# Loading part of one tile in transfers of 12, 8, 8, 4 and 96 partitions in a DMA-bound gradient kernel

## The chip, the core and the metric

The kernel runs on one core of a Trainium2 chip. The metric is the device time of one execution in microseconds; the lower, the better. A core has compute engines (here VectorE, called DVE, and GpSimd, called POOL, do the arithmetic), a sync engine SP that issues the transfers, and 16 DMA engines that move data between the device memory (HBM) and the on-chip memory (SBUF, 128 partitions).

## What is computed

```python
x = randn(8192, 8192).astype(float32)
return np.gradient(x, axis=1)
```

Along each row of 8192 numbers, an inner element of the result is half the difference of its right and left neighbours. The first and the last element of a row are plain differences: second minus first, and last minus last but one. Input and output have 268.4 MB each.

## The kernel before

The 8192 rows are cut into `nsets` = 32 tiles (sets) of 256 rows. A partition holds `R` = 2 neighbouring rows of one tile, one after the other: `W` = 16384 numbers, 64 KB. So a tile is 128 partitions of 64 KB, 8.39 MB, and is contiguous in HBM (L36 and L37). There are `NB` = 3 buffers in SBUF, `slot0` to `slot2` (L40); tile i uses slot i % 3. The input is put `SH` = 64 numbers from the start of the buffer and the result is written from its start, so that the result of a tile takes the place of its input.

For each tile the steps are these.

- **Load**, `load(i)` (L58 to L61): one DMA of the whole tile, issued by SP (L60). From tile 3 on it waits for the store of the tile that had the same slot, `stores[i - NB]`.
- **Row ends** (L70): POOL takes the one-sided differences at the two ends of each row, 128 x 4 numbers, into the small tile `ends`. It waits for the load.
- **Inner elements** (L76): one DVE instruction over the whole tile, 128 x 16382, halves the differences of neighbours. It waits for the row ends, because it overwrites the input.
- **Placing the ends** (L87): DVE or, in 12 of the 32 tiles, POOL copies the row ends into the result.
- **Store** (L89): one DMA of the whole tile, issued by SP. It waits for the placing.

All loads and stores are issued by SP, in the order in which the program has them: loads 0, 1, 2, then stores 0, 1, 2, loads 3, 4, 5, stores 3, 4, 5 and so on, up to loads 30 and 31 and stores 30 and 31 (L91 to L93 issue the next three loads after each third store). An instruction that waits at SP holds those behind it. The order is written out by hand (`tc.manual_schedule()`), and `chain` (L45) tells the framework which waits each step needs: the named steps, and the instruction before it on its engine where both belong to the same slot. Each transfer reports its completion on one of eight semaphores, which are taken in turn; a transfer that takes a semaphore again also waits for the transfer that had it eight issues earlier.

Of the kernel before, what the change touches and what calls it, by code (L numbers as in the profile page):

```python
# [1 line left out]

# [4 lines left out]


@with_exitstack
def kernel(  # L10
    ctx: ExitStack,
    tc: tile.TileContext,
    x: bass.AP,
    out: bass.AP,
):

    nc = tc.nc
    P = nc.NUM_PARTITIONS
    n, m = x.shape
    R = 2
    NB = 3  # L30
    SH = 64
    W = R * m
    nsets = n // (P * R)
    f32 = x.dtype

    x_sets = x.rearrange("(s p t) m -> s p (t m)", p=P, t=R)  # L36
    out_sets = out.rearrange("(s p t) m -> s p (t m)", p=P, t=R)  # L37

    pool = ctx.enter_context(tc.tile_pool(name="pool", bufs=1))
    slots = [pool.tile([P, SH + W], f32, name=f"slot{k}", tag=f"slot{k}") for k in range(NB)]  # L40
    ends = pool.tile([P, nsets, R, 2], f32, name="ends", tag="ends")
    loads, stores = [], [None] * nsets
    in_front = {}

    def chain(i, ins, *needed):  # L45

        group, engine = f"slot{i % NB}", ins.ins.engine
        keep = [o.ins for o in needed]  # L50
        if in_front.get(engine, (None,))[0] == group:
            keep.append(in_front[engine][1])
        tc.declare_no_dep(ins.ins, group=group, keep=keep, reason="implied by the needed step")
        tc.add_to_no_dep_group(group, ins.ins)
        in_front[engine] = group, ins.ins
        return ins

    def load(i):  # L58
        b = slots[i % NB]
        ins = nc.sync.dma_start(out=b[:, SH : SH + W], in_=x_sets[i])  # L60
        loads.append(chain(i, ins, *([stores[i - NB]] if i >= NB else [])))  # L61

    with tc.manual_schedule():
        for i in range(NB):
            load(i)
        for i in range(nsets):
            b = slots[i % NB]
            xin = b[:, SH : SH + W].rearrange("p (t m) -> p t m", m=m)

            ins = nc.gpsimd.tensor_sub(  # L70
                out=ends[:, i, :, :],
                in0=xin[:, :, 1 : m : m - 2],
                in1=xin[:, :, 0 : m - 1 : m - 2],
            )
            at = [chain(i, ins, loads[i])]
            ins = nc.vector._custom_dve(  # L76
                dve_ops.TENSOR_TENSOR_REDUCE_SUB_MAX,
                out=b[:, 1 : W - 1],
                in0=b[:, SH + 2 : SH + W],
                in1=b[:, SH : SH + W - 2],  # L80
                s0=0.0,
                s1=0.5,
            )
            halved = chain(i, ins, *at)
            res = b[:, 0:W].rearrange("p (t m) -> p t m", m=m)
            placer = nc.gpsimd if i % 5 in (1, 3) and i < nsets - 2 else nc.vector
            ins = placer.tensor_copy(out=res[:, :, 0 : m : m - 1], in_=ends[:, i, :, :])  # L87
            placed = chain(i, ins, halved)
            ins = nc.sync.dma_start(out=out_sets[i], in_=b[:, 0:W])  # L89
            stores[i] = chain(i, ins, placed)  # L90
            if i % NB == NB - 1:  # L91
                for k in range(i + 1, min(i + 1 + NB, nsets)):
                    load(k)  # L93


# [1 line left out]
_INS = ['x']  # L97
_OUTS = [((8192, 8192), 'float32')]


# [23 lines left out]
```

## Time and profile before

| | |
|---|---|
| median of 3 runs | 1247.86 us (1247.71 to 1247.9) |
| span of the profiled execution | 1245.7 us |
| HBM read and written | 268.44 MB each |
| L76, DVE, 32 times | 551.2 us, 17.224 us each |
| L70, POOL, 32 times | 6.3 us, 0.198 us each |
| L87, DVE 20 times, POOL 12 times | 3.4 us and 2.3 us |
| loads, L60, 32 times | 0.339 us to issue; 58.0 us from issue to landing (median) |
| stores, L89, 32 times | 0.343 us to issue; 40.4 us from issue to landing (median) |
| loads 0, 1 and 2 have landed at | 22.7, 42.0 and 62.4 us |

The span goes from the first to the last instruction in the profile; the times of the runs are measured from outside and are some 2 us longer. A transfer's time to landing includes its time in the queue behind earlier transfers. The trace also holds a record for each DMA packet: its start, its duration and its size, but not the DMA engine that it ran on. A load or a store of a whole tile leaves 128 packets of 65,536 bytes (one for each partition) and 16 of 4 bytes, which report the completion of each of the 16 engines.

### The profile page before, as it was taken

To read this page: it belongs to the slowest core of one execution; us is meant where nothing else is said; L and a number is where in the kernel's file an instruction comes from. 1 tells how busy PE (TensorE), PEld (TensorE's weight loads), DVE (VectorE), ACT (ScalarE), POOL (GpSimd) and SP (SyncE) were. 2 spreads that over 40 slices of the span, in tenths; PEclk is the share of its full clock that TensorE was granted. 3 is DMA by queue.
4 is the path that set the end of the run, shared out by engine and by line. 5 is a ranking of instruction groups with operands and counts; after the bars stand their busy time and mean duration, and the time that the engine had idled before them with its cause. 6 is when DMAs were issued, how large, how long until landed. Compare 5 with 4: busy or idle time off the path is not lost.

```text
span 1245.7 us, 237 instructions
## 1 busy us (share of the span) xinstructions
DVE 554.6 (45%) x52; POOL 8.8 (1%) x48
## 2 busy tenths in 40 slices
DVE  2850583069009702850582079009603840591083
POOL 0000000000000000000000000000000000000000
DMA  9999999999999999999999999999999999999999
GB/s 404 438 436 423 427 431 438 438 438 436 436 427 431 425 438 436 425 434 436 429 434 436 434 436 434 436 434 438 419 436 436 434 438 438 431 434 429 429 410 404
DMA packets 9217, 536.88 MB, mean 431 GB/s; under 512 B 1024, under 2 KB 1024, under 8 KB 1024
## 3 DMA queue, kind: packets, MB, share of 16 engines
q1 hardware_dynamic: 9216, 536.88, 99.8%
q14 instruction: 1, 0.01, 0.0%
HBM read 268.44 MB, written 268.44 MB: 431 GB/s over the span
## 4 chain that ended last, share of the span: by engine, by line
another core or an unknown queue 74%; DVE 18%; DMA 3%; issue 2%; POOL 1%; SPq 0%; POOLq 0%
DVE slot L76 18%; DMA slot<-in_x_dram 3%; POOL ends L70 0%; POOL slot L87 0%; SPq L60 0%; POOLq L119 0%; DVE slot L87 0%
## 5 line engine op out<-in xcount | busy, mean ns | idle before, releaser
L76 DVE CUSTOM_DVE_ANT_0 slot<-slot 128x16382 f32<-128x16382 f32 x32 | 551.2, 17224 | 668.7 <-POOL ends L70 668.7
L70 POOL TENSOR_TENSOR ends<-slot 128x4 f32<-128x4 f32 x32 | 6.3, 198 | 989.6 <-DMA slot<-in_x_dram 989.6
L87 POOL COPY slot<-ends 128x4 f32<-128x4 f32 x12 | 2.3, 190 | 207.9 <-DVE slot L76 207.9
L87 DVE COPY slot<-ends 128x4 f32<-128x4 f32 x20 | 3.4, 172 | 0.7
L108 POOL MEMSET const-bfloat16-1.0<- 128x1 bf16 x1 | 0.1, 101 | 0.0
L108 POOL MEMSET const-uint8-127<- 128x1 uint8 x1 | 0.1, 101 | 0.0
L108 POOL MEMSET const-float32-0.0<- 128x1 f32 x1 | 0.1, 98 | 0.2 <-issue 0.2
L108 POOL MEMSET const-float32-1.0<- 128x1 f32 x1 | 0.1, 98 | 0.0
## 6 DMA issues: line engine op xcount, KB each, us to landing
slot<-in_x_dram SPq DMA_DIRECT2D x32, 58.0
out_dram<-slot SPq DMA_DIRECT2D x32, 40.4
```

Of the source, the lines that this page charges most:

```text
L70: ins = nc.gpsimd.tensor_sub(out=ends[:, i, :, :], in0=xin[:, :, 1 : m : m - 2], in1=xin[:, :, 0 : m - 1 : m - 2],)
L76: ins = nc.vector._custom_dve(dve_ops.TENSOR_TENSOR_REDUCE_SUB_MAX, out=b[:, 1 : W - 1], in0=b[:, SH + 2 : SH + W], in1=b[:, SH : SH + W - 2],
L87: ins = placer.tensor_copy(out=res[:, :, 0 : m : m - 1], in_=ends[:, i, :, :])
L108: nc = _bacc.Bacc("TRN2", target_bir_lowering=False, num_devices=1)
```

## The change

Tile 2, the third, is loaded in six transfers instead of one. The last `STEP` = 4096 columns of its 16384 (16 KB of the 64 KB in each partition) are cut off and loaded by five transfers, of partitions 0 to 11, 12 to 19, 20 to 27, 28 to 31 and 32 to 127. A sixth transfer loads the first 12288 columns (48 KB) of all 128 partitions. They are issued by SP in this order, in the place where the one load of tile 2 was. POOL's first step on tile 2 waits for all six. All other tiles are loaded as before, in one transfer, and the stores and the arithmetic are the same.

```diff
+    STEP = 4096
...
     def load(i):
         b = slots[i % NB]
-        ins = nc.sync.dma_start(out=b[:, SH : SH + W], in_=x_sets[i])
-        loads.append(chain(i, ins, *([stores[i - NB]] if i >= NB else [])))
+        after = [stores[i - NB]] if i >= NB else []
+        parts = []
+        whole = W
+        if i == NB - 1:
+            whole = W - STEP
+            first = 0
+            for k in (12, 8, 8, 4, 96):
+                parts.append((slice(first, first + k), slice(whole, W)))
+                first += k
+        parts.append((slice(0, P), slice(0, whole)))
+        loads.append([])
+        for rows, cols in parts:
+            ins = nc.sync.dma_start(
+                out=b[rows, SH + cols.start : SH + cols.stop], in_=x_sets[i][rows, cols]
+            )
+            loads[i].append(chain(i, ins, *after))
...
-            at = [chain(i, ins, loads[i])]
+            at = [chain(i, ins, *loads[i])]
```

The instructions of DVE and POOL and their order are the same in both programs. SP has 69 transfers instead of 64.

## The prediction

> **What bounds the kernel now.** I read the page first, then the chain of waits, the timeline of the last 60 us, the DMA view of a narrow window there, and last the DMA packets one by one. The page:
>
> ```profile
> span 1245.7 us, 237 instructions
> ...
> DVE 554.6 (45%) x52; POOL 8.8 (1%) x48
> ...
> DMA  9999999999999999999999999999999999999999
> GB/s 404 438 436 423 427 431 438 438 438 436 436 427 431 425 438 436 425 434 436 429 434 436 434 436 434 436 434 438 419 436 436 434 438 438 431 434 429 429 410 404
> DMA packets 9217, 536.88 MB, mean 431 GB/s; under 512 B 1024, under 2 KB 1024, under 8 KB 1024
> ...
> q1 hardware_dynamic: 9216, 536.88, 99.8%
> ```
>
> The reader should see that nothing but the 16 DMA engines is busy throughout. The 9216 packets are 64 transfers (32 loads, 32 stores) of 144: 128 rows of 64 KB and 16 completion writes of 4 bytes, so 8 rows and one completion for each engine. An engine's whole work is 512 rows; the packets' median is 2.418 us, hence 512 x 2.418 = 1238.0 of the 1245.7 us. An engine takes its packets in the order of issue, and a lost microsecond comes back nowhere unless the engine idles later. The end of the chain of waits, and the timeline there:
>
> ```profile
> 1109.87 77.00 another core or an unknown queue
> 1186.87 0.07 issue
> 1186.93 0.20 POOL ends L70
> 1187.13 19.11 issue
> ```
>
> ```profile
> 1186.93 0.20 POOL L70 TENSOR_TENSOR ends<-slot 128x4 f32<-128x4 f32 x1 [77.07 <-DMA slot<-in_x_dram]
> 1187.17 17.22 DVE L76 CUSTOM_DVE_ANT_0 slot<-slot 128x16382 f32<-128x16382 f32 x1 [59.84 <-POOL ends L70]
> 1204.42 0.17 DVE L87 COPY slot<-ends 128x4 f32<-128x4 f32 x1
> 1204.62 19.69 SPq L89 DMA_DIRECT2D out_dram<-slot  x2
> ```
>
> Load 30 lands at 1186.87, DVE works 17.22 us, and store 30 is issued at 1204.62. Meanwhile the engines have only load 31 (19.35 us) to do. The DMA view of 1200 to 1208 us, in slices of 0.2 us that count a packet where it starts:
>
> ```profile
> DMA  0997799000900970070000000009070000000009
> GB/s 0 983 1638 328 328 655 655 0 0 0 655 0 0 655 328 0 0 328 0 0 0 0 0 0 0 0 0 4915 0 328 0 0 0 0 0 0 0 0 0 3604
> ...
> q1 hardware_dynamic: 63, 3.08, 89.4%
> ```
>
> The last rows of load 31 start spread over 3 us, yet 15 rows of store 30 start together near 1205.5 (4915 GB/s x 0.2 us / 65,536 B = 15) and one later. The 15 engines had run dry. The packet records name no engine, but a packet begins where the one before it on its engine ended, so 16 streams can be followed (rough where two coincide). At load 31's end they lag the earliest by 0, 0.04, 0.14, 0.17, 0.18, 0.28, 0.62, 0.79, 0.90, 0.90, 1.63, 1.64, 2.25, 2.41, 2.61 and 3.05 us, 1.10 on average; at load 2's end the spread was only 0.64. The last stream never idles and alone sets the end: its lag enters load 30's landing and so store 30. After the restart come two stores, 2 x 19.35 us, from 1205.5 to 1244.3, and completion. Hence the rule of my sum: **the time moves by the change of the largest lag.** Perfect shares would gain 3.05 - 1.10 = 1.95 us and no more.
>
> **The change, part by part.** Issue: SP gets five more issues, 5 x 0.34 us (median of L60) = 1.7 us. They come after loads 0 and 1 are issued and load 0 lands at 22.7, so two whole loads cover them; store 0, behind them in SP's queue, waits until 40.4 anyway. Uncovered they would cost 1.7. POOL's step for tile 2 now waits for six landings instead of one; at 0.017 us for a semaphore event on SP that is 0.1 us, in a tile whose store is issued at 80.1, about 20 us before store 1 ends on the engines. DMA semaphores go round among eight, so five more transfers change which older transfer each SP instruction also waits for. It is always the transfer eight issues back, which is done before the slot's own wait ends: 0. Compute is unchanged.
>
> Shares: the last 16 KB of each of tile 2's 128 rows are cut off. I take a transfer of k<=12 rows to put one row on each of the first k engines and that of 96 rows to put six on each; this is an assumption from the change's wording. Engines 0-3 then get 10 pieces, 4-7 get 9, 8-11 get 7, 12-15 get 6, instead of 8. [...]
>
> The price of a 16 KB piece is the unknown, as the trace holds no data packet under 64 KB.
> - Lower bound: time goes with bytes, 2.418 / 4 = 0.605 us. The lags change by +1.21, +0.60, -0.60 and -1.21 us for the four groups.
> - Upper bound: a small transfer of 12, 8, 8 or 4 rows holds its engines as long as the shortest data packet seen, 2.418 us, because several engines start in step on neighbouring rows instead of each on eight of its own. Engines 0-3: 4 x 2.418 + 6 x 0.605 - 8 x 0.605 = +8.46; engines 4-7, three such pieces: +6.04; engines 8-11, one: +1.21; engines 12-15: -1.21.
>
> The nearest rows are the packets that started in step: the 16 first ones took 3.02 us on average and the 16 that started near 58.2 us 3.52, so 0.6 and 1.1 us above 2.418. A small piece at 0.605 plus 1.1 would be 1.7, nearer to 2.418 than to 0.605. I take the upper bound.
>
> [...]
>
> Which stream is which engine: in order of their first packets (1.75 to 2.43 us), as if engines were started in number order, the largest lags are 0.62 (engines 0-3), 2.41 (4-7), 0.90 (8-11) and 3.05 (12-15). Upper sum: 0.62 + 8.46 = 9.08; 2.41 + 6.04 = 8.45; 0.90 + 1.21 = 2.11; 3.05 - 1.21 = 1.84. The largest goes from 3.05 to 9.08, **+6.0 us**. Lower sum: 1.83, 3.01, 0.30 and 1.84, so 3.01 against 3.05, **0.0 us**.
>
> One credit: between 60 and 1203 us the streams lose 2.23 us each in packets over 2.435 us, in bursts where all engines pass from loads to stores within a microsecond. Engines 6 to 9 us behind no longer meet the others there; I credit half, 1.1 us (bounds 0 and 2.2). Sum: 6.0 - 1.1 = +4.9. The late tile 2 costs nothing else: landing at 70 instead of 62.4, it is computed at 88 and its store queues behind store 1, which the engines finish at 100; that cover would be gone from about 12 us of lag. The profiled execution becomes 1245.7 + 4.9 = 1250.6; the runs' median lies 2.2 us above that span, outside the first and last instruction, so I predict **1252.8 us**.
>
> **Rivals.**
> 1. Bytes alone count: 1247.9, and between 1247.86 - 1.21 and + 1.21 as streams and engines pair otherwise. For it: 2.418 us holds in loads and stores alike, as if the engine set it. Against it: packets in step took up to 3.8.
> 2. The shares fit: the slow streams are engines 12-15 alone, the fast ones 0-3. Then the largest lag falls by the 1.21 us taken off: 1246.65. For it: the 3.05 and a 2.61 belong to streams that started late. Against it: 2.41 and 2.25 started fifth and seventh and would get more.
> 3. The bursts vanish: the shifted engines lose none of the 2.23 us and the shares fit too: 1247.86 - 2.2 - 1.2 = 1244.4. It needs pieces at the price of their bytes, which leaves a shift of only 2.4 us, less than the bursts' and the streams' present spread of 3 us.
> 4. The change doesn't do what it says: each small transfer runs on one engine. That gets 32 + 6 - 8 = 30 pieces more, 18.2 us; from a lag of 0.62 the largest becomes 18.8, +15.7: 1263.6. Nothing in the trace excludes it but the diff's description.
>
> **How the numbers follow.** Forecast 0.54, rival 1 0.24, rival 2 0.14, rival 3 0.05, rival 4 0.03. The low end is rival 2's 1246.6. The high end drops the credit (+6.0) and lets the six pieces of the 96-row transfer cost a fifth of the way from 0.605 to 2.418, 6 x 1.81 / 5 = 2.2: +8.2, 1256.1. Left out are rivals 3 and 4 and some of the forecast's tail. The forecast's own range is 1250.4 to 1256.1. About what a measurement can tell from no change is 0.2%, 2.5 us: slower means above 1250.36, which the forecast and rival 4 give, 0.57; rivals 1 and 2 are the same, 0.38; rival 3 is faster, 0.05.
>
> **What would show it.** Right: the 16 KB packets of the small transfers take well over 0.605 us; tile 2's landing moves from 62.4 to some 68 to 71 us; the landing of load 30 moves from 1186.9 to about 1192; load 31's last packets spread over some 9 us, with most engines idle longer before store 30. Rival 1 or 2: pieces at 0.6 us and a landing of load 2 within 1.5 us of 62.4. Wrong altogether: a new wait at SP before store 0 or load 3, or the streams' lags at load 31 not being those at load 2 plus the old drift.

## The result, and the profile after

The changed kernel takes 1255.22 us (median of 5 runs, 1254.77 to 1256.04) against 1247.86 us before: 7.4 us more, a ratio of 1.0059 with an interval of 1.0049 to 1.007. The profiled execution has a span of 1252.7 us against 1245.7, 7.0 us more.

From the page of the changed kernel:

```profile
span 1252.7 us, 250 instructions
...
GB/s 404 313 440 435 433 435 435 435 435 435 433 433 433 435 433 423 435 433 429 435 433 435 435 435 435 435 435 433 433 435 435 435 431 435 433 416 435 435 412 402
DMA packets 9393, 536.88 MB, mean 429 GB/s; under 512 B 1072, under 2 KB 1072, under 8 KB 1072
...
q1 hardware_dynamic: 9392, 536.88, 99.8%
```

The bytes are the same and the DMA engines are as busy as before, 99.8%, yet one slice of 31.3 us, the second, moves 313 GB/s instead of 438. The packets also say how the new transfers were spread. There are 48 more completion writes (1072 - 1024): a single load has 16, the six transfers have 64, and 12 + 8 + 8 + 4 + 16 + 16 = 64. Each small transfer ran on as many engines as it has partitions.

Where the slice loses its time is seen when stretches of 5 us are laid side by side. The columns are the stretch, DVE's and POOL's busy time, the granted clock, the busy share of the DMA engines and what they moved (a packet counts whole where it starts, so a share can come out a little over 1). First the kernel before, then the changed one:

```profile
core 0: us, DVE busy (x) POOL busy (x), PEclk, DMA share, GB/s
42.00:47.00 5.00, 4.73 (x1) 0.20 (x1) 1.00 0.97 419
47.00:52.00 5.00, 5.00 (x1) 0.00 (x0) 1.00 0.97 419
```

```profile
42.00:47.00 5.00, 4.23 (x1) 0.20 (x1) 1.00 1.11 154
47.00:52.00 5.00, 5.00 (x1) 0.00 (x0) 1.00 0.99 187
```

The engines are busy and move less than half. A busy DMA engine is one that has a packet under way, not one that moves data at its rate. In the packet records the 128 pieces of 16 KB take 0.615 to 2.431 us, 1.55 on average, where a quarter of a 64 KB packet would be 0.605. The timeline shows what that does to tile 2, in POOL's steps:

```profile
42.54 0.20 POOL L74 TENSOR_TENSOR ends<-slot 128x4 f32<-128x4 f32 x1 [19.78 <-DMA slot<-in_x_dram]
60.06 0.19 POOL L91 COPY slot<-ends 128x4 f32<-128x4 f32 x1 [17.32 <-DVE slot L80]
71.82 0.20 POOL L74 TENSOR_TENSOR ends<-slot 128x4 f32<-128x4 f32 x1 [11.57 <-DMA slot<-in_x_dram]
```

Tile 2's first step starts at 71.82 instead of 62.44 us, 9.4 us later. The end of the timeline, which answers to the one shown of before:

```profile
1194.02 17.22 DVE L80 CUSTOM_DVE_ANT_0 slot<-slot 128x16382 f32<-128x16382 f32 x1 [59.88 <-POOL ends L74]
1211.28 0.17 DVE L91 COPY slot<-ends 128x4 f32<-128x4 f32 x1
1211.48 19.69 SPq L93 DMA_DIRECT2D out_dram<-slot  x2
```

DVE starts on tile 30 at 1194.02 instead of 1187.17, and the rest follows 6.9 us later than before. So 9.4 us were lost at one place near the start, about 2.4 of them came back on the way, and 7 reached the end.

### The profile page after: what moved, and what is told of

Same layout as the page of the kernel before. It is cut to its first block, busy times and chain, and to the rows that moved or that the text cites. A ratio compares the mean times of both kernels' runs of the same rounds, so it can differ in the third digit from the quotient of the medians.

```text
span 1252.7 us, 250 instructions
## 1 busy us (share of the span) xinstructions
DVE 554.6 (44%) x52; POOL 8.8 (1%) x48
## 2 busy tenths in 40 slices
DMA packets 9393, 536.88 MB, mean 429 GB/s; under 512 B 1072, under 2 KB 1072, under 8 KB 1072
## 3 DMA queue, kind: packets, MB, share of 16 engines
q1 hardware_dynamic: 9392, 536.88, 99.8%
## 4 chain that ended last, share of the span: by engine, by line
another core or an unknown queue 75%; DVE 17%; DMA 3%; issue 3%; POOL 1%; SPq 0%; POOLq 0%
DVE slot L80 17%; DMA slot<-in_x_dram 3%; POOL ends L74 0%; POOL slot L91 0%; SPq L62 0%; POOLq L123 0%; DVE slot L91 0%; POOLq L74 0%
```

## The experiments

In what follows "landing" is the start of POOL's first step on tile 2 (62.4 us before, 71.8 in the changed kernel). Times are medians, the difference is to runs of the kernel before on the same chip, and the interval is that of the ratio.

**Is it the cut, the shares, or the neighbours?** Four kernels cut the same 4096 columns off tile 2 and differ in the rows of the transfers.

Equal shares, one transfer:

```diff
-            for k in (12, 8, 8, 4, 96):
+            for k in (128,):
```

> Tile 2's last 4096 columns come in one transfer of 128 partitions ahead of the other 12288 columns: the cut is there, the shares are equal and every engine has the partitions of an ordinary load. Theory A (engines that write neighbouring partitions at the same time share a path, so small pieces are dear): the 16 KB packets take about 0.61 us, load 2 lands near 62.4 us, time 1247.9 +- 0.7. Theory B (the unequal number of pieces is what costs): the same, 1247.9. Theory C (cutting a 64 KB row into 16 and 48 KB is what costs): packets of 1.0 to 2.4 us as in the changed kernel, landing near 71, time near 1255.

Measured: 1248.03 us, -0.1 us (0.9991 to 1.001); the pieces take 0.612 us on average, 0.645 at most. Two transfers of 16 KB and 48 KB rows are as good as one of 64 KB. Theory C falls.

```profile
42.00:47.00 5.00, 4.71 (x1) 0.20 (x1) 1.00 1.11 478
47.00:52.00 5.00, 5.00 (x1) 0.00 (x0) 1.00 1.09 472
```

Equal shares, two halves:

```diff
-            for k in (12, 8, 8, 4, 96):
+            for k in (64, 64):
```

> The last 4096 columns come in two transfers of 64 partitions, 0 to 63 and 64 to 127: 4 + 4 pieces for each of the 16 engines, equal shares. [...] Theory B: equal shares cost nothing, 1247.9. Theory C: near 1255.

Measured: 1252.54 us, +4.4 us (1.0025 to 1.0051); landing 67.05; pieces 1.27 us in the median, 1.20 on average, twice 0.612. Every engine has as many pieces as in the run above, and still the first stretch moves about half (216 against 478 GB/s). That is against theory B: equal shares are not enough. Why a piece of a transfer of 64 partitions takes twice as long as one of a transfer of 128 is not shown.

```profile
42.00:47.00 5.00, 4.13 (x1) 0.20 (x1) 1.00 1.02 216
47.00:52.00 5.00, 5.00 (x1) 0.00 (x0) 1.00 1.09 288
```

Four transfers of 8 neighbours, and four of 8 partitions 4 apart, both with the transfer of 96:

```diff
-            for k in (12, 8, 8, 4, 96):
+            for k in (8, 8, 8, 8, 96):
```

```diff
-            first = 0
-            for k in (12, 8, 8, 4, 96):
-                parts.append((slice(first, first + k), slice(whole, W)))
-                first += k
+            for j in range(4):
+                parts.append((slice(j, 32, 4), slice(whole, W)))
+            parts.append((slice(32, P), slice(whole, W)))
```

> Four transfers of 8 neighbouring partitions (0 to 7, 8 to 15, 16 to 23, 24 to 31) and one of 96: engines 0 to 7 get 10 pieces, 8 to 15 get 6. Theory A: about as the changed kernel, pieces over 1 us, landing 69 to 72, time 1253 to 1256. Theory B: the two pieces more cost 2 x 0.605 = 1.2 us at most, 1247.9 to 1249.1. Theory C: near 1255.

> The same counts of pieces as the run with four transfers of 8 neighbours, but each of the four takes every fourth partition of 0 to 31, so that its 8 engines write partitions 4 apart. Theory A: the pieces of these four take about 0.61 us and only the transfer of 96 partitions stays dear, landing 2 to 5 us earlier than with neighbours, time 2 to 5 us less. Theories B and C: no difference between the two.

Measured with neighbours: 1256.28 us, +8.2 us (1.0055 to 1.0085), landing 72.0. Measured 4 apart: 1251.89 us, +3.8 us (1.0018 to 1.004), landing 67.4. Same bytes, same number of transfers, same pieces for every engine, 4.4 us apart: what decides is which partitions are written at the same time, or which input rows are read; the next two kernels tell these apart. First the stretches with neighbours, then those 4 apart:

```profile
42.00:47.00 5.00, 3.76 (x1) 0.20 (x1) 1.00 1.12 141
47.00:52.00 5.00, 5.00 (x1) 0.00 (x0) 1.00 1.08 206
```

```profile
42.00:47.00 5.00, 3.85 (x1) 0.20 (x1) 1.00 1.11 279
47.00:52.00 5.00, 5.00 (x1) 0.00 (x0) 1.00 1.11 288
```

The pieces of the four transfers are not all at 0.61 as expected of theory A: the first twelve packets to start take 0.62 us on average, but the first 32 take 0.81 and the others 1.08. The engines that have only pieces of the transfer of 96 are in it from the start (in the changed kernel four streams begin it at 41.34 to 41.48 us, while the others begin their small pieces at 40.96 to 41.47); that their pieces slow the others was not tested by itself.

**Partitions or rows in HBM?** Neighbouring partitions were also neighbouring input rows. Two kernels part them. They are the kernel with partitions 4 apart, with a third slice in each of the four entries that names the input rows to read (the lines that use it are left out here):

```diff
+                parts.append((slice(j, 32, 4), slice(whole, W), slice(8 * j, 8 * j + 8)))
```

```diff
+                parts.append((slice(8 * j, 8 * j + 8), slice(whole, W), slice(j, 32, 4)))
```

> The four transfers of 8 write every fourth partition of 0 to 31 but read 8 neighbouring rows of the input, so the last 4096 columns of these 32 rows of tile 2 end up in other partitions (the output has them permuted). If the shared way is at the partitions (SBUF side): as the run with every fourth partition, landing near 67.4, time near 1252. If neighbours in HBM are what costs: as the run with neighbours, landing near 72, time near 1256.

> The reverse: the four transfers of 8 write 8 neighbouring partitions but read every fourth input row (the output is permuted in the same rows). SBUF side: landing near 72, time near 1256. HBM side: landing near 67.4, time near 1252.

Measured: partitions 4 apart, 1250.88 us, +3.2 us (1.0017 to 1.0037), landing 67.35. Neighbouring partitions, 1255.96 us, +8.2 us (1.0051 to 1.0081), landing 71.7. The loss goes with the partitions that are written, not with the input rows that are read. First the stretches with partitions 4 apart, then those with neighbouring partitions:

```profile
42.00:47.00 5.00, 4.34 (x1) 0.20 (x1) 1.00 1.21 305
47.00:52.00 5.00, 5.00 (x1) 0.00 (x0) 1.00 1.03 269
```

```profile
42.00:47.00 5.00, 2.95 (x1) 0.20 (x1) 1.00 1.03 141
47.00:52.00 5.00, 5.00 (x1) 0.00 (x0) 1.00 1.11 220
```

**Bytes or a fixed price for each transfer?**

```diff
-    STEP = 4096
+    STEP = 2048
```

and 8192 in a second kernel.

> The changed kernel with 2048 instead of 4096 columns cut off: pieces of 8 KB. Theory A (shared way into neighbouring partitions, so the loss goes with the bytes that are loaded in such transfers): half of the 9.4 us, load 2 lands near 67.1 us, time 1250 to 1252.5. Theory D (a fixed price for each of the five added transfers): landing near 71.8, time near 1255.

> The changed kernel with 8192 columns cut off: pieces of 32 KB. Theory A: twice 9.4 us, load 2 lands near 81 us, time 1262 to 1266. Theory D: as the changed kernel, near 71.8 and 1255.

Measured: 2048 columns, 1249.74 us, +2.0 us (1.0008 to 1.0027), landing 65.6; 8192 columns, 1266.24 us, +18.5 us (1.0132 to 1.0166), landing 84.8. The landing is late by 3.2, 9.4 and 22.4 us. A fixed price is out. Strict proportion is not right either: I expected 4.7 and 18.8, the time with 2048 columns lies 0.3 us under the range that I gave, that with 8192 columns 0.2 us over it. Each doubling adds more than it should, as if some 3 us were always saved. One part of that is seen: the last 16 packets of load 2 are slow in the kernel before (they start near 58 us and take 3.52 us instead of 2.42, 1.1 us for each engine), and in these kernels they take the ordinary time of their size (1.82 us for the 48 KB of the changed one). The rest lies in the pieces: those of 8 KB took 0.62 us on average, 2.1 times the 0.302 of their bytes, those of 16 KB 1.55 us, 2.6 times 0.605. Why is open. The stretches with 8192 columns:

```profile
42.00:47.00 5.00, 3.64 (x1) 0.20 (x1) 1.00 0.87 105
47.00:52.00 5.00, 5.00 (x1) 0.00 (x0) 1.00 0.86 105
```

**Unequal shares without neighbours.** These kernels are the kernel before with extra loads into a spare tile `spare` (128 x 3072, its definition is left out here), ahead of load 2. Eight loads of 8 partitions:

```diff
+            if i == 1:
+                for j in (0, 1, 2, 3, 32, 33, 34, 35):
+                    nc.sync.dma_start(out=spare[j : j + 29 : 4, :], in_=x_sets[0][j : j + 29 : 4, 0:3072])
```

> The kernel before with extra work: ahead of load 2, eight loads of 8 partitions 4 apart (0 to 63 in all, 12 KB each) into a spare tile that nobody reads: 96 KB more, 96 / 64 x 2.418 = 3.63 us, for engines 0 to 7 alone, each on partitions of its own. This prices unequal shares without neighbours. Theory A: the 12 KB packets take 0.45 us; the largest lag grows by 3.0 to 3.6 us, less up to 2.3 that the stagger saves in the bursts: 1248.6 to 1251.7. If small transfers are dear for any other reason (their number, 8 engines at a time), packets well over 0.45 us and 1252 or more.

Measured: 1252.05 us, +3.7 us (1.0017 to 1.0038). It does not answer the question. There are eight completion semaphores; the seventh and eighth extra load take those of loads 0 and 1 and wait for them. SP's list of waits has this line, which the kernel before has not:

```profile
SPq L69 <- DMA slot<-in_x_dram: 35.6, 2, 18.7
```

Load 2, behind them in SP's queue, was issued at 42.69 instead of within the first 2.1 us, after load 1 had landed, and in the packet records only 8 of the 16 engines had a packet under way from 42.5 to 43.5 us. I repeated it with five loads, which need no old semaphore.

One extra load for all engines alike:

```diff
+            if i == 1:
+                nc.sync.dma_start(out=spare[:, :], in_=x_sets[0][:, 0:3072])
```

> The kernel before with one extra load of 128 partitions x 12 KB into a spare tile ahead of load 2: 3.63 us more for all 16 engines alike, no stagger. Every theory: load 2 lands 3.6 us later and the time grows by 3.6, to 1251.5 to 1251.9. Against the run that loads engines 0 to 7 alone: if stagger saves bursts, that one is faster by 1 us or more; if not, they are within 0.6 us.

Measured: 1251.68 us, +3.3 us (1.0016 to 1.0035), landing 66.3, as expected; the comparison with the spoilt run says nothing.

Five extra loads, of partitions 4 apart, and of neighbours:

```diff
+                for j in (0, 1, 2, 3, 32):
+                    nc.sync.dma_start(out=spare[j : j + 29 : 4, :], in_=x_sets[0][j : j + 29 : 4, 0:3072])
```

```diff
+                for j in (0, 1, 2, 3, 4):
+                    nc.sync.dma_start(out=spare[8 * j : 8 * j + 8, :], in_=x_sets[0][8 * j : 8 * j + 8, 0:3072])
```

> The kernel before with extra work: ahead of load 2, five loads of 8 partitions 4 apart, 12 KB each, into a spare tile that nobody reads. Engines 0 to 7 alone get 60 KB more, 60 / 64 x 2.418 = 2.27 us, each on partitions away from the others'; no transfer waits for an older one. This is the price of unequal shares without neighbours (the earlier run with eight loads had its eighth wait for load 1). Theory A: packets near 0.46 us; load 2 lands 2.3 us later, at 64.7; if the streams that end last are among engines 0 to 7 the time grows by up to 2.3, if all of them are among 8 to 15 by nothing: 1248 to 1250.6. If small transfers of 8 are dear as such: over 1 us a packet, 1252 or more.

> The same extra bytes, engines and number of loads, but each of the five takes 8 neighbouring partitions (0 to 7, 8 to 15 and so on to 39). [...] Any theory in which only the shares, the sizes or the number of transfers count: the same as the run with partitions 4 apart, within 0.6 us.

Measured 4 apart: 1249.79 us, +1.4 us (1.0002 to 1.002), landing 64.5; the 40 packets take 0.460 to 0.465 us, within 0.02 us of the 0.453 of their bytes. Measured with neighbours: 1251.91 us, +3.5 us (1.002 to 1.0046), landing 67.9; the packets take 1.15 us on average and 1.70 at most. Here first the kernel with loads 4 apart, then the one with neighbours:

```profile
42.00:47.00 5.00, 4.71 (x1) 0.20 (x1) 1.00 1.10 476
47.00:52.00 5.00, 5.00 (x1) 0.00 (x0) 1.00 0.97 419
```

```profile
42.00:47.00 5.00, 3.00 (x1) 0.20 (x1) 1.00 0.80 169
47.00:52.00 5.00, 5.00 (x1) 0.00 (x0) 1.00 0.82 341
```

So a transfer on 8 engines is not dear as such, nor are shares of 60 KB more for half of the engines dear beyond their bytes. What was dear were loads of 8 neighbouring partitions: 1.15 us for a packet of 12 KB, against 0.46 with partitions 4 apart. That engines hinder each other at neighbouring partitions is my reading of this; no record names the engine or the partition of a packet. How far apart the partitions must be was not measured: only neighbours and partitions 4 apart were compared.

The loss also reaches engines that have none of these pieces. With neighbours, the 8 engines without extra loads go straight on to the 64 KB packets of load 2; their first ones, begun between 41.1 and 42.7 us, took 5.8 to 6.6 us instead of 2.42. With loads 4 apart no 64 KB packet that began then took over 2.43. How they are slowed is not shown.

## Why the prediction came out as it did

The direction and the range held: 1255.22 lies in 1246.6 to 1256.1, and the likeliest case was the one that came. The predicted 1252.8 was 2.4 us short, and that it came so near is in part luck: its terms have errors of both signs, and the rule by which they were put together did not hold.

- **What bounds the kernel** held. The engines' own streams set the end; in the changed kernel load 31's streams still end 3.1 us apart, and store 30 is issued 17.7 us after POOL's step on tile 30, as before.
- **Issue and waits at nothing** held. The last part of tile 2 was issued by 4.0 us (SP's group of eight loads lasts from 0.74 to 3.97), and store 0 was issued at 40.25 against 40.40. A wait of SP for a load is new in the list of its first 45 us. The prediction had named a new wait before store 0 as a sign of being altogether wrong; it costs nothing, because the wait for DVE ends later:

```profile
SPq L93 <- DMA slot<-in_x_dram: 20.4, 2, 18.5
SPq L93 <- DVE slot L91: 17.7, 1, 17.7
```

- **The price of a piece** was right in kind, as pieces took 1.55 us on average against the 0.605 of their bytes, but the sizes were wrong. I put 2.418 us on the 32 pieces of the small transfers and 0.605 on the 96 pieces of the large one. Told apart by the completion records that follow them, they took 1.65 (2.20 at most) and 1.52 us on average. The failed term is the second: I let the dear transfer of 96 rows into the high end of the range alone, at a fifth of the way from 0.605 to 2.418, where it came out at half of it. It is three quarters of the pieces and cost 96 x (1.52 - 0.605) / 16 = 5.5 us for each engine on average. The 32 small ones cost 32 x (1.65 - 0.605) / 16 = 2.1. The 16 KB pieces were not all, either: the packets of 48 KB that began while other engines were still in the pieces took up to 3.54 us instead of 1.82, another 1.3 us for each engine. Less the 1.1 us that the last packets of load 2 no longer lose, this makes 7.8 us, and 7.8 us is what the streams are late on average at the end of load 2.
- **Lags by group** failed with it. Engines 12 to 15 were to end load 2 earlier by 1.21 us. In the completion records the first stream ends load 2 at 68.3 and the last at 71.2, against 61.4 and 62.1: all are late, by 6.9 to 9.1 us. The assumed shares were right: followed from packet to packet, four streams have 10 pieces, four 9, four 7 and four 6, and they end them near 56, 54.7, 52.6 and 51.5 us; which engine has which number no record shows. But the pieces were dear on all engines, and the streams that were through first met the slow 48 KB packets. I expected a spread of some 9 us at load 31; it is 3.1. By its letter, the rule "the time moves by the change of the largest lag" gives +0.1 us (from 3.05 to 3.14), where the span grew by 7.0: it measures lags against the earliest stream, and that one moved too.
- **The late tile 2 costs nothing else** held, but not its limit of about 12 us of lag. With 8192 columns load 2 landed 22.4 us late, and from 84 to 145 us the engines still had a busy share of 1.00 and moved 432 GB/s: stores 0 and 1 stand behind load 2 and are late with it, so they still cover tile 2.
- **The credit for bursts** was near its size, but it was not all that came back. The packets over 2.435 us between 100 us and load 31 cost 2.23 us for each engine before and 1.43 in the changed kernel: 0.8 us against the 1.1 credited, and the streams' average lateness fell from 7.8 us at load 2 to 7.0 at load 31. Of the 9.1 us of the last stream, 6.85 were left there, so it got 2.3 back. The difference is drift: from load 2 to load 31 the last stream falls behind the average of the streams by another 1.6 us in the kernel before (0.34 to 1.95) and by 0.2 in the changed one (1.65 to 1.82). The prediction had no term for this. With 8192 columns the slow packets cost 0.03 us, and there 22.4 us of lateness at load 2 became 18.5 of span; with 60 KB more for half of the engines, 4 apart, they cost 3.26, and with one transfer of 128, which shifts no engine, 2.63. These are single profiles; that stagger is what saves the bursts fits the large shifts and not the small one, and stays unproved.
- **The rivals.** Bytes alone (1) fell with the 1.55 us of a piece. Fitting shares (2) and vanishing bursts (3) gave no gain, but both suppose pieces at the price of their bytes, which was not met. Whether such shares gain at that price was not tried: the run with five loads 4 apart, slower by a ratio of 1.0002 to 1.002, gives eight engines more bytes and takes none from the others. One engine for each small transfer (4) is excluded by the 48 completions.

## What to carry to other kernels

In these runs a piece of 16 KB took 0.612 us on average in a transfer of 128 partitions, 1.20 in two of 64, and in the changed kernel 1.52 in the one of 96 and 1.65 in those of 12, 8, 8 and 4 neighbours. What slows them is not shown. These numbers speak for whole transfers of 128 partitions. In this kernel a tile could be cut by columns at no cost that shows (0.9991 to 1.001 with rows of 16 and 48 KB), but not by partitions; where that must be, small transfers of partitions 4 apart were cheaper than neighbours, by 4.4 us here. Judge a stretch by the bytes that it moves, not by the busy share of its DMA engines, which was 0.99 to 1.11 where 154 to 187 GB/s went through.

## What the runs showed of the hardware that was not expected

- A transfer of 96 partitions on 16 engines is dear too: 1.52 us on average for a 16 KB piece, and still 1.18 for the pieces that began after the small transfers had ended (48.9 us), against 0.612 in a transfer of 128.
- Packets of an ordinary pattern were slow while dear pieces were under way on other engines: those of 48 KB took up to 3.54 us instead of 1.82, and beside the extra loads of neighbours those of 64 KB up to 6.58 us instead of 2.42.
- With 8192 columns in such transfers, the stretch from 42 to 52 us moved 105 GB/s, a quarter of the 419 of before.
